# Turning blocks of an encoder's mixers by 32x32 squares through HBM in place of TensorE

## The chip, the core and the metric

The kernel runs on one core of a Trainium2 chip. The metric is the device time of one execution in microseconds (us); a comparison uses the median of several executions. The engines are TensorE (PE in the profile, its weight loads PEld), VectorE (DVE), ScalarE (ACT), GpSimd (POOL), and SyncE (SP), which here only issues transfers. Each engine works through its own queue in order; an instruction that waits holds up all that stands behind it on that engine.

## What is computed

A trunk of two layers over 256 tokens of width 2048, in float32. With `h = rms_norm(x)`, cut to what matters:

```python
# layer 0: retention (8 heads) and neighbourhood attention (8 heads), one input projection
rq, rk, rv, rg, nq, nk, nv = split(h @ w_in_ab, 7)
ret = rms_norm(retention(rq, rk, rv), ret_g) * silu(rg)
na = attention(rms_norm(nq, na_q_g), rms_norm(nk, na_k_g), nv, rpb)
x = x + concat(ret, na) @ w_out_ab
# layer 1: differential attention (8 heads, two softmax maps each)
q, k, v = split(h @ w_in_c, 3)
x = x + diff_attention(rms_norm(q, q_g), rms_norm(k, k_g), v) @ w_out_c
# both layers: 4-head cross-attention into 256 memory tokens, then a SwiGLU FFN of width 5632
k, v = split(rms_norm(mem) @ w_kv, 2);  q = rms_norm(x) @ w_q
x = x + attention(rms_norm(q, xq_g), rms_norm(k, xk_g), v) @ w_o
g, u = split(rms_norm(x) @ w_ffn_in, 2);  x = x + (silu(g) * u) @ w_ffn_out
```

## The kernel before

**Products.** Every large product is done by `gemm` (L297). A float32 operand is split into a high part that TensorE takes as it is (`hi`, `wh`) and a rest (`lo`, `wl`), and three matmuls make a product: `hi x wh`, `hi x wl`, `lo x wh` (L321 to L323). The stationary side is the activation with its features on the partitions, 16 k-tiles of 128 features by 256 tokens, as a `pair` of two tiles (L212). The moving side are the weights in blocks of 512 columns.

**The unit of work** is half a weight load: two k-tiles for two halves of the tokens, 12 matmuls of 512 columns. A block of 512 output columns takes 8 units when it contracts over 2048. `prepare` (L269) readies units ahead: SP loads a 1 MB block of weights into `raw` (three buffers, two units each), ScalarE casts it to `wh` (L292), VectorE subtracts to get `wl` (L293), three buffers of each. So a unit is cast when TensorE is done with the one three units earlier. All 864 units are in one list, so that weights of the next product are readied during the last units of the one before.

**The epilogues.** When a block's last unit is issued, `epi` takes its two accumulators (256 tokens on the partitions by 512 columns). For a query or a key with a norm, `normed_T` (L481): ScalarE squares (L470), VectorE sums by head (L471), POOL takes the power -1/2 (L334), VectorE scales to `z` (L475). For one without a norm, `plain_T` (L496): ScalarE copies with the token's scale (`evac`, L451). For a gate (L652, L653): silu and a product with the retention's output give `sg`. The accumulators have two buffers, so a block waits for the epilogue two blocks before.

**Turning.** What comes out has tokens on the partitions; scores and output projections need features there. TensorE turns a block of 512 features by `turn` (L340): four 128x128 transposes against an identity into one PSUM bank, twice for a block; after each, `gained_pair` (L442) on ScalarE (`hi`, times a gain) and VectorE (`lo`). `heads_T` (L459) does it for queries and keys, `gate_T` (L607) for the gates. A second way is `regroup` (L377), used before the change for the residual stream (`feed`, L409) and for the FFN's activations (`act_T`, L830): VectorE transposes 32x32 squares within the partitions (L389, two instructions), SP stores the 512 KB to a buffer `zd` in HBM (L391), POOL loads it back in four pieces that put the squares in their places (L394), and ScalarE and VectorE split it into `hi` and `lo`.

**The order by hand.** Everything beside the units is a generator in `Side` (L33). After each unit `pump` runs one step (in two of the products, two) of the first task in the list that is due; a step's `yield n` sets it due n units later. At most `CAP` tasks are begun and unfinished at a time. `drain` runs tasks until the given ones are done, where a product needs their output. In `regroup` the loads come `LAND` = 2 units after the squares, and the splitting `MOVE` = 5 units after them. A key's or query's turn comes 4 units after its epilogue, a plain one's 3, a gate's 2. Heads (`attend` L548, `ret_head` L581, `diff_head` L662) start when the queries and the keys of their group are both turned.

**Order of blocks.** Neighbourhood groups (query, key, value blocks, twice), retention groups (twice), two gate blocks; in layer 1 four groups of query, key and value. The first two blocks of a mixer are woven into each other, so that they end two units apart; from the third on a block follows the other. In the cross-attention the memory's keys come first, then the queries, then the values.

**Buffers.** Large pairs live in two places, A and B, that change roles: `hT` in one and the mixer's output `oT` in the other. `qT` and `kT` are turned queries and keys, `m8` a shared place for the bias, the retention's output and the cross-attention's output.

Of the kernel before, what the change touches and what calls it, by code (L numbers as in the profile page):

```python
# [16 lines left out]
P = 128  # L17
# [8 lines left out]
NEG = -1e30  # L26
LAND, MOVE = 2, 5
FFN_GROUPS = ((0, 4), (4, 8), (8, 11))
# [4 lines left out]
class Side:  # L33

    CAP = 5

# [43 lines left out]
def trunk_kernel(  # L82
# [214 lines left out]
    def gemm(kts, src, epi, gate=None, steps=1, wide=False):  # L297
        hi, lo = src
        w2, rows, cols, order = plan[at["phase"]]
# [3 lines left out]
        for b, u in order:  # L303
# [13 lines left out]
            for t in range(2):  # L317
                ts = slice(t * P, (t + 1) * P)
                for j in range(2):
                    kt = kts[u // 2] + 2 * (u % 2) + j  # L320
                    nc.tensor.matmul(acc[t], lhsT=hi[:, kt, ts], rhs=wh[:, j], start=first and j == 0, stop=False)  # L321
                    nc.tensor.matmul(acc[t], lhsT=hi[:, kt, ts], rhs=wl[:, j], start=False, stop=False)  # L322
                    nc.tensor.matmul(acc[t], lhsT=lo[:, kt, ts], rhs=wh[:, j], start=False, stop=last and j == 1)  # L323
            if last:
# [23 lines left out]
    def gained(dst, kt, src, g):  # L348
        hi, lo = dst[0][:, kt], dst[1][:, kt]
# [26 lines left out]

    def regroup(srcs, room=""):  # L377


        if room == "m8":  # L380
            both = m8.tile([P, 2, 4 * T], F32, tag="m8", name="zz")
            zt, zT = both[:, 0], both[:, 1]
        elif room:
            zt, zT = (qk.tile([P, 4 * T], F32, tag=room + x, name="zz") for x in "hl")
        else:
            zt, zT = (vp.tile([P, 4 * T], F32, tag="v" + x, name="zz") for x in "hl")
        zt = zt.rearrange("p (j k t b) -> p j k t b", j=4, k=4, t=2)
        for t in range(2):
            nc.vector.transpose(zt[:, :, :, t], srcs[t].rearrange("p (k j a) -> p j k a", j=4, a=32))  # L389
        zd = dram.tile([4, 32, 4, T], F32, name="zd")  # L390
        nc.sync.dma_start(zd.rearrange("i a j n -> (i a) (j n)"), zt.rearrange("p j k t b -> p (j k t b)"))  # L391
# [17 lines left out]
    def feed(dst, b, srcs, gi, layer, ssr, room):  # L409
# [5 lines left out]
        for k in range(4):  # L415
            g = gain(gi, layer, 4 * b + k)
            hi, lo = (x[:, 4 * b + k].rearrange("p (t i b) -> p t i b", t=2, i=4) for x in dst)
# [6 lines left out]
    def feed_x(dst, b, gi, layer, ssr, room=""):  # L424

        return [side.add(feed(dst, b, x_block(b), gi, layer, ssr, room))] * 2
# [31 lines left out]

    def heads_T(zs, dst, g):  # L459
        for u in range(2):  # L460
# [19 lines left out]

    def normed_T(acc, rstd, gc, name, wait=4):  # L481
        r1, r2 = rstd
# [10 lines left out]
        d = turned(name)  # L493
        return d, side.add(heads_T(zs, d, head_gain(gc)), wait)

    def plain_T(acc, rstd, name, mul):  # L496
        zs = evac(acc, rstd)
        d = turned(name)
        return d, side.add(heads_T(zs, d, mul), 3)

# [47 lines left out]
    def attend(g, h, dst, kt, bias=None):  # L548
# [15 lines left out]
        for s in range(2):  # L564
            product(po, part(v, s, slice(h * HD, (h + 1) * HD)), part(pT, s), s == 0, s == 1)
        split(dst[0][:, kt], dst[1][:, kt], po)

# [38 lines left out]

    def gate_T(zs, oT, kt, g):  # L607
        for u in range(2):
            pt = turn(zs, u)
            gained_pair(part(oT, slice(kt + 2 * u, kt + 2 * u + 2)), pt, g)  # L610
            yield 0

    def retention_na(j, hT, rstd, oT, gate):
        groups = [{"n": 0} for gi in range(4)]
        groups[0]["tb"] = side.add(na_bias(j, 0, groups[0], hT[0][:, 4, 0:16].bitcast(F32)), 6)
        tails = []

        def epi(b, acc):
            if b < 12:
                gi, part = b // 3, b % 3  # L620
                g = groups[gi]
                if gi < 2:
                    if part == 0:
                        g["q"], g["tq"] = normed_T(acc, rstd, c_naq + j, "qT")
                    elif part == 1:
                        g["k"], g["tk"] = normed_T(acc, rstd, c_nak + j, "kT")
                        side.drain([g["tb"], small[0]])
                        heads = [side.add(attend(g, h, oT, 8 + gi * 4 + h, bias=g["bias"]), cond=prepared(g))
                                 for h in range(4)]
# [15 lines left out]
            else:  # L645
# [4 lines left out]
                for t in range(2):  # L650
# [108 lines left out]
    for layer in range(2):  # L759
# [36 lines left out]
        ssr = new_ss("ssx")  # L796
        tasks = [t for b in range(4) for t in feed_x(hT, b, 1, layer, ssr, ("", "", "qT", "m8")[b])]
# [14 lines left out]
        xo = m8.tile([P, 2, 4, T], F32R, tag="m8", name="xo")  # L812
        xo = (xo[:, 0], xo[:, 1])
        heads = [side.add(attend(g, h, xo, h), cond=prepared(g)) for h in range(4)]
# [5 lines left out]
        def epi_xo(b, acc):  # L820
# [3 lines left out]
            else:  # L824
                tasks.extend(feed_x(hT, b, 3, layer, ssr, ("", "", "qT", "kT")[b]))

# [3 lines left out]
        def act_T(aT, zs, kt):  # L830
            zT = yield from regroup(zs)
            for t in range(2):
                split(*(x[:, kt:kt + 4, t * P:(t + 1) * P].rearrange("p k (i b) -> p k i b", i=4) for x in aT),
                      zT[:, :, :, t].rearrange("p i k b -> p k i b"))

# [75 lines left out]
```

## Time and profile before

| | |
|---|---|
| median of 3 runs | 2475.36 us (2473.93 to 2477.48) |
| the profiled execution | 2475.84 us |
| its span, first to last instruction | 2474.1 us |
| TensorE, share of the span busy | 99% |
| VectorE, ScalarE, POOL | 60%, 48%, 6% |
| transfers, mean share of 16 DMA engines busy | 4 to 8 tenths in the slices of the page |
| moved | 511.82 MB, 207 GB/s |

How to read its rows: "L345 PE MATMUL pt<-ident,z" is line, engine, operation, tile written and tiles read. Behind a group stand its count, its busy time in us, the mean in ns of one instruction, and the idle time of the engine just before, with what ended it. A row of the timeline begins with its start and its length in us (two merged instructions, x2, have one length for both). A row of waits is: engine and line, what it waited for, then us in all, times, the longest. Matmuls overlap in the pipeline, so their lengths are longer than the steps between their starts. The lines that matter most here are L345 (turns), L389 to L394 (squares) and L292/L293 (weights).

### The profile page before, as it was taken

The numbers are of one execution on the slowest core, as the hardware profiler recorded it, in microseconds if no ns is written. First come the engines' busy times: TensorE is split into PE (matmuls) and PEld (weight loads), VectorE is DVE, ScalarE is ACT, GpSimd is POOL, SyncE is SP. The second block draws the span as 40 slices with busy tenths as digits, with TensorE's granted clock in tenths as the row PEclk, the third lists the DMA queues.
The fourth block names the chain that finished last, engine by engine and source line by source line (L and its number), as shares of the span: only waits on it lengthen the run. The fifth ranks groups of instructions, "written<-read, shape, count | busy, mean of one in ns | idle before, by whom it ended". The sixth has DMA issues, their size and how long they took to land.

```text
span 2474.1 us, 28641 instructions
## 1 busy us (share of the span) xinstructions
PE 2456.3 (99%) x11184; PEld 2037.1 (82%) x11184; DVE 1475.7 (60%) x1833; ACT 1187.0 (48%) x1538; POOL 138.2 (6%) x215
## 2 busy tenths in 40 slices
PE   8999999999999999999999999999999999999999
PEld 6888888888888888888888888888888888888887
DVE  6775565675655555555567766767655545555554
ACT  6554464564443444444455555655544444443443
POOL 1000001010000000000010000010100000000000
PEclk9999999999999999999999999999999999999999
DMA  8555567656765666566674555675766656665665
GB/s 288 177 169 179 175 226 245 214 192 213 233 216 200 205 212 225 194 198 226 225 241 164 170 170 168 212 249 171 237 222 210 215 188 214 228 206 200 207 217 175
DMA packets 250184, 511.82 MB, mean 207 GB/s; under 512 B 11328, under 2 KB 11968, under 8 KB 250048
## 3 DMA queue, kind: packets, MB, share of 16 engines
q1 hardware_dynamic: 239568, 484.47, 58.5%
q0 software_dynamic: 8320, 23.08, 4.1%
q10 hardware_dynamic: 2160, 2.44, 0.3%
q8 instruction: 87, 1.43, 0.2%
q14 instruction: 49, 0.40, 0.0%
HBM read 486.88 MB, written 23.07 MB: 206 GB/s over the span
## 4 chain that ended last, share of the span: by engine, by line
PE 92%; DMA 3%; DVE 3%; ACT 1%; POOL 1%; issue 0%; ACTq 0%; SPq 0%; POOLq 0%; DVEq 0%
PE acc L322 30%; PE acc L321 30%; PE acc L323 30%; DMA zz<-zd 2%; DVE wl L293 1%; DMA zd<-zz 1%; PE pt L345 1%; ACT wh L292 0%; PE pt L545 0%; PE pa_s L437 0%; PE pa_s L436 0%; DVE x_sb L741 0%; PE pa_s L435 0%; POOL zz L394 0%; PE pa_r L595 0%
## 5 line engine op out<-in xcount | busy, mean ns | idle before, releaser
L293 DVE TENSOR_TENSOR wl<-raw,wh 128x1024 fp32r<-128x1024 f32 (+1 forms) x865 | 1053.7, 1221 | 870.8 <-ACT wh L292 870.4
L292 ACT CAST wh<-raw 128x1024 fp32r<-128x1024 f32 (+1 forms) x865 | 909.1, 1051 | 1158.2 <-PE acc L323 1132.8
L322 PE MATMUL acc<-wl,hTfh 128*128 128x512 f32 x1408 | 547.9, 389 | 0.6 <-DVE wl L293 0.6
L323 PE MATMUL acc<-wh,hTfl 128*128 128x512 f32 x1408 | 547.7, 389 | 0.0
L321 PE MATMUL acc<-wh,hTfh 128*128 128x512 f32 x1408 | 547.7, 389 | 0.0
L321 PE MATMUL acc<-wh,hTh 128*128 128x512 f32 x832 | 332.0, 399 | 9.8 <-ACT wh L292 8.3
L322 PE MATMUL acc<-wl,hTh 128*128 128x512 f32 x832 | 325.7, 391 | 0.9 <-DVE wl L293 0.9
L323 PE MATMUL acc<-wh,hTl 128*128 128x512 f32 x832 | 325.8, 392 | 0.0
L322 PEld LDWEIGHTS acc<-wl,hTfh 128*128 128x128 f32 x1408 | 264.3, 188 | 56.2 <-DVE wl L293 1.4
L323 PEld LDWEIGHTS acc<-wh,hTfl 128*128 128x128 f32 x1408 | 264.3, 188 | 54.9
L321 PEld LDWEIGHTS acc<-wh,hTfh 128*128 128x128 f32 x1408 | 264.3, 188 | 54.9
L322 PE MATMUL acc<-wl,aTh 128*128 128x512 f32 x704 | 274.0, 389 | 0.2 <-DVE wl L293 0.2
L323 PE MATMUL acc<-wh,aTl 128*128 128x512 f32 x704 | 273.9, 389 | 0.0
L321 PE MATMUL acc<-wh,aTh 128*128 128x512 f32 x704 | 273.9, 389 | 0.0
L321 PEld LDWEIGHTS acc<-wh,hTh 128*128 128x128 f32 x832 | 157.2, 189 | 40.0 <-ACT wh L292 8.3
L323 PEld LDWEIGHTS acc<-wh,hTl 128*128 128x128 f32 x832 | 156.7, 188 | 34.0
L322 PEld LDWEIGHTS acc<-wl,hTh 128*128 128x128 f32 x832 | 157.2, 189 | 31.2 <-DVE wl L293 1.8
L394 POOL DMA_DIRECT2D zz<-zd x160 | 87.3, 552 | 1589.9 <-DMA zd<-zz 1410.9
L322 PEld LDWEIGHTS acc<-wl,aTh 128*128 128x128 f32 x704 | 132.1, 188 | 28.2 <-DVE wl L293 0.8
L321 PEld LDWEIGHTS acc<-wh,aTh 128*128 128x128 f32 x704 | 132.1, 188 | 27.5
L323 PEld LDWEIGHTS acc<-wh,aTl 128*128 128x128 f32 x704 | 132.1, 188 | 27.3
L321 PE MATMUL acc<-wh,oTh 128*128 128x512 f32 x256 | 100.2, 392 | 0.0
(189 smaller groups left out, 1940.3 us busy)
## 6 DMA issues: line engine op xcount, KB each, us to landing
raw<-in_w_ffn_in SPq DMA_DIRECT2D x176, 1024.0 KB, 5.1
raw<-in_w_ffn_out SPq DMA_DIRECT2D x88, 1024.0 KB, 5.1
raw<-in_w_in_ab SPq DMA_DIRECT2D x55, 1024.0 KB, 5.2
raw<-in_w_in_c SPq DMA_DIRECT2D x48, 1024.0 KB, 5.2
zd<-zz SPq DMA_DIRECT2D x40, 512.0 KB, 3.8
zz<-zd POOLq DMA_DIRECT2D x160, 128.0 KB, 5.4
raw<-in_w_out_ab SPq DMA_DIRECT2D x16, 1024.0 KB, 5.1
raw<-in_w_xkv SPq DMA_DIRECT2D x16, 1024.0 KB, 5.0
```

Source lines behind the costliest of these rows:

```text
L292: nc.scalar.copy(wh[:, js], raw[:, rs])
L293: nc.vector.tensor_sub(wl[:, js], raw[:, rs], wh[:, js])
L321: nc.tensor.matmul(acc[t], lhsT=hi[:, kt, ts], rhs=wh[:, j], start=first and j == 0, stop=False)
L322: nc.tensor.matmul(acc[t], lhsT=hi[:, kt, ts], rhs=wl[:, j], start=False, stop=False)
L323: nc.tensor.matmul(acc[t], lhsT=lo[:, kt, ts], rhs=wh[:, j], start=False, stop=last and j == 1)
L345: nc.tensor.transpose(pt[:, j, t * P:(t + 1) * P], srcs[t][:, c:c + P], ident)
L394: nc.gpsimd.dma_start(zT[32 * j:32 * j + 32].rearrange("a (i n) -> a i n", i=4), zd[:, :, j].rearrange("i a n -> a i n"))
```

## The change

Twelve blocks go from `turn` to `regroup`: the neighbourhood queries (2), the retention queries (2), the differential queries (4), the gates (2) and the memory's keys (one in each layer). The other keys, the cross-attention's queries, the probabilities and the heads' outputs are still turned by TensorE.

- The moved blocks begin in the step right after their epilogue (a wait of 0 in place of 4, 3 or 2 units), and their splitting comes `SLOW` = 8 units after the squares; where there is a gain, ScalarE multiplies the landed block by it in place first. The loads still come after 2 units.
- The squares lie in a free place: for the mixers' queries the block of the output pair that is written last or not yet (`oT`'s block 0 in layer 0, block 3 in layer 1), for the gates `qT` and `kT`, for the memory's keys `qT`.
- So that a quarter of a pair can be lent, a pair becomes four blocks of four k-tiles, each a tile of its own (`Pair`), and the kernel addresses k-tiles by `at`.
- `CAP` goes from 5 to 6 tasks.

```diff
-LAND, MOVE = 2, 5
+LAND, MOVE, SLOW = 2, 5, 8
...
-    CAP = 5
+    CAP = 6
...
-    def pair(which, name):
-        hi = big.tile([P, 16, T], F32R, tag=f"{which}h", name=f"{name}h")
-        lo = big.tile([P, 16, T], F32R, tag=f"{which}l", name=f"{name}l")
-        return hi, lo
+    class Pair:
...
+        def __init__(self, which, name):
+            self.which, self.name, self.blocks = which, name, {}
+
+        def blk(self, b):
+            if b not in self.blocks:
+                self.blocks[b] = tuple(big.tile([P, 4, T], F32R, tag=f"{self.which}{x}{b}", name=f"{self.name}{x}")
+                                       for x in "hl")
+            return self.blocks[b]
+
+        def at(self, kt, n=None):
+            k = kt % 4
+            return tuple(x[:, k if n is None else slice(k, k + n)] for x in self.blk(kt // 4))
...
+    def room_for(room):
...
+        if room in ("qT", "kT"):
+            return tuple(qk.tile([P, 4 * T], F32, tag=room + x, name="zz") for x in "hl")
+        return tuple(big.tile([P, 4 * T], F32, tag=room[0] + x + room[1], name="zz") for x in "hl")
+
+    def regroup(srcs, room="v", wait=MOVE):
...
         yield LAND
         for j in range(4):
             nc.gpsimd.dma_start(zT[32 * j:32 * j + 32].rearrange("a (i n) -> a i n", i=4),
                                 zd[:, :, j].rearrange("i a n -> a i n"))
-        yield MOVE - LAND
+        yield wait - LAND
         return zT.rearrange("p (i k t b) -> p i k t b", i=4, k=4, t=2)
+
+    def split_moved(dst, zT):
+
+        for t in range(2):
+            split(*(x[:, :, t * P:(t + 1) * P].rearrange("p k (i b) -> p k i b", i=4) for x in dst),
+                  zT[:, :, :, t].rearrange("p i k b -> p k i b"))
...
-    def heads_T(zs, dst, g):
+    def heads_T(zs, dst, g, room=None):
+        if room:
+            zT = yield from regroup(zs, room, wait=SLOW)
+            if g is not None:
+                flat = zT.rearrange("p i k t b -> p (i k t b)")
+                nc.scalar.activation(flat, flat, AF.Copy, scale=g)
+            split_moved(dst, zT)
+            return
         for u in range(2):
             pt = turn(zs, u)
             gained_pair(part(dst, slice(2 * u, 2 * u + 2)), pt, g)
...
-        return d, side.add(heads_T(zs, d, head_gain(gc)), wait)
+        return d, side.add(heads_T(zs, d, head_gain(gc), room), 0 if room else 4)
...
-        return d, side.add(heads_T(zs, d, mul), 3)
+        return d, side.add(heads_T(zs, d, mul, room), 0 if room else 3)
...
-    def gate_T(zs, oT, kt, g):
-        for u in range(2):
-            pt = turn(zs, u)
-            gained_pair(part(oT, slice(kt + 2 * u, kt + 2 * u + 2)), pt, g)
-            yield 0
+    def gate_T(zs, oT, kt, g, room):
+        yield from heads_T(zs, oT.at(kt, 4), g, room)
...
+        spare = oT.which + "0"
...
-                        g["q"], g["tq"] = normed_T(acc, rstd, c_naq + j, "qT")
+                        g["q"], g["tq"] = normed_T(acc, rstd, c_naq + j, "qT", spare)
...
-                    g["q"], g["tq"] = plain_T(acc, rstd, "qT", 1.0)
+                    g["q"], g["tq"] = plain_T(acc, rstd, "qT", None, spare)
...
-                tails.append(side.add(gate_T(zs, oT, gi * 4, head_gain(c_ret + j)), 2))
+                tails.append(side.add(gate_T(zs, oT, gi * 4, head_gain(c_ret + j), ("qT", "kT")[gi])))
...
+        spare = oT.which + "3"
...
-                g["q"], g["tq"] = normed_T(acc, rstd, c_dq + j, "qT")
+                g["q"], g["tq"] = normed_T(acc, rstd, c_dq + j, "qT", spare)
...
-            g["k"], g["tk"] = normed_T(acc, mssr[1:], c_xk + layer, "kT")
+            g["k"], g["tk"] = normed_T(acc, mssr[1:], c_xk + layer, "kT", "qT")
```

More of the change, by code (lines that the diff above doesn't have):

```diff
@@ L319, in gemm @@
                 for j in range(2):
[L320 to L323, printed above, removed]
+                    hi, lo = src.at(kts[u // 2] + 2 * (u % 2) + j)
+                    nc.tensor.matmul(acc[t], lhsT=hi[:, ts], rhs=wh[:, j], start=first and j == 0, stop=False)
+                    nc.tensor.matmul(acc[t], lhsT=hi[:, ts], rhs=wl[:, j], start=False, stop=False)
+                    nc.tensor.matmul(acc[t], lhsT=lo[:, ts], rhs=wh[:, j], start=False, stop=last and j == 1)
             if last:
@@ L479, in turned, with normed_T @@
         return tuple(qk.tile([P, 4, T], F32R, name=name + x) for x in "hl")
-    def normed_T(acc, rstd, gc, name, wait=4):
+    def normed_T(acc, rstd, gc, name, room=None):
         r1, r2 = rstd
@@ L627, in epi @@
                         side.drain([g["tb"], small[0]])
-                        heads = [side.add(attend(g, h, oT, 8 + gi * 4 + h, bias=g["bias"]), cond=prepared(g))
+                        heads = [side.add(attend(g, h, oT, 8 + gi * 4 + h, g["bias"]), cond=prepared(g))
                                  for h in range(4)]
@@ L796, in trunk_kernel @@
         ssr = new_ss("ssx")
-        tasks = [t for b in range(4) for t in feed_x(hT, b, 1, layer, ssr, ("", "", "qT", "m8")[b])]
+        tasks = [t for b in range(4) for t in feed_x(hT, b, 1, layer, ssr, ("v", "v", "qT", "m8")[b])]
         g = {"wait": 3}
         def epi_k(b, acc):
-            g["k"], g["tk"] = normed_T(acc, mssr[1:], c_xk + layer, "kT")
+            g["k"], g["tk"] = normed_T(acc, mssr[1:], c_xk + layer, "kT", "qT")
         def epi_q(b, acc):
@@ L812, in trunk_kernel @@
         xo = m8.tile([P, 2, 4, T], F32R, tag="m8", name="xo")
-        xo = (xo[:, 0], xo[:, 1])
+        heads_out = pair("", "xo")
+        heads_out.blocks[0] = (xo[:, 0], xo[:, 1])
+        xo = heads_out
         heads = [side.add(attend(g, h, xo, h), cond=prepared(g)) for h in range(4)]
@@ L824, in epi_xo @@
             else:
-                tasks.extend(feed_x(hT, b, 3, layer, ssr, ("", "", "qT", "kT")[b]))
+                tasks.extend(feed_x(hT, b, 3, layer, ssr, ("v", "v", "qT", "kT")[b]))
         gemm((0,), xo, epi_xo, gate={0: heads[:2], 1: heads[2:]}, steps=2)
@@ L831, in act_T @@
             zT = yield from regroup(zs)
-            for t in range(2):
-                split(*(x[:, kt:kt + 4, t * P:(t + 1) * P].rearrange("p k (i b) -> p k i b", i=4) for x in aT),
-                      zT[:, :, :, t].rearrange("p i k b -> p k i b"))
+            split_moved(aT.at(kt, 4), zT)
         for g0, g1 in FFN_GROUPS:
```

30 lines of the change are left out of this document (14 added, 16 removed).

## The prediction

> **What bounds the kernel now.** I read the page's busy times first, then the chain that ended last, then what TensorE waited for, and only then single places in the timeline. From the page, part 1 and part 4:
>
> ```profile
> PE 2456.3 (99%) x11184; PEld 2037.1 (82%) x11184; DVE 1475.7 (60%) x1833; ACT 1187.0 (48%) x1538; POOL 138.2 (6%) x215
> ...
> PE 92%; DMA 3%; DVE 3%; ACT 1%; POOL 1%; issue 0%; ACTq 0%; SPq 0%; POOLq 0%; DVEq 0%
> ```
>
> TensorE is busy 99% of the span and carries 92% of the chain. Of the waits of its weight loads, the largest that comes more than once:
>
> ```profile
> PEld acc L322 <- DVE wl L293: 5.0, 7, 0.9
> ```
>
> So its weight loads wait for VectorE's `wl`, the low halves of the weights, 5.0 us in 7 places, and no more. An instruction taken off TensorE shortens the run by what it holds TensorE, as long as `wl` does not get late in its place. That condition is what this prediction is about. How the weights pace ScalarE, by its timeline:
>
> ```profile
> 1364.41 1.05 ACT L292 CAST wh<-raw 128x1024 fp32r<-128x1024 f32 x1 [1.18 <-PE acc L323]
> 1367.13 1.05 ACT L292 CAST wh<-raw 128x1024 fp32r<-128x1024 f32 x1 [1.67 <-PE acc L323]
> ```
>
> A cast starts when TensorE frees a buffer, every 2.72 us: one unit of 12 matmuls, so 0.227 us a matmul. Beside its cast ScalarE has 1.67 us free in a unit.
>
> **What goes.** The turns by TensorE, by the view of line 345:
>
> ```profile
> L345 PE MATMUL pt<-ident,z x160: 270/272/273, 58.9 to 1706.1; 128*128 128x128 f32 x160
> L345 PEld LDWEIGHTS pt<-ident,sg x16: 138/140/142, 337.0 to 363.4; 128*128 128x128 f32 x16
> L345 PE MATMUL pt<-ident,sg x16: 270/272/273, 337.2 to 363.5; 128*128 128x128 f32 x16
> ```
>
> These durations overlap in the pipeline, so what a group of four costs is read from TensorE's timeline around one (a query of the differential layer):
>
> ```profile
> 1369.42 0.39 PE L323 MATMUL acc<-wh,hTl 128*128 128x512 f32 x1
> 1369.65 0.60 PE L345 MATMUL pt<-ident,z 128*128 128x128 f32 x4
> 1370.01 0.48 PE L321 MATMUL acc<-wh,hTh 128*128 128x512 f32 x1
> 1370.32 0.39 PE L322 MATMUL acc<-wl,hTh 128*128 128x512 f32 x1
> ```
>
> From L323 to the next unit's L322 pass 0.90 us; two undisturbed steps are 0.45 us; the group costs 0.45 us (0.447 before rounding). The change moves twelve blocks: neighbourhood queries 2, retention queries 2, differential queries 4, gates 2, memory keys 2. Each is two groups of four: 24 groups, 96 of these 176 transposes. **Saved on TensorE: 24 x 0.447 = 10.7 us.**
>
> **What comes.** The nearest rows are those of the activations, which take this very way already:
>
> ```profile
> L389 DVE STREAM_TRANSPOSE zz<-sg 128x512 f32<-128x512 f32 x44 | 28.5, 685 | 0.0
> L430 DVE TENSOR_TENSOR aTl<-zz,aTh 128x512 fp32r<-128x512 f32 x44 | 28.3, 685 | 0.0
> ...
> L447 DVE SCALAR_TENSOR_TENSOR kTl<-pt,gcol,kTh 128x512 fp32r<-128x512 f32 x16 | 11.9, 745 | 0.0
> ```
>
> A moved block gives VectorE two square transposes (685 ns) and two subtractions (685) for two fused ones (745): 2.74 for 1.49 us, 15 us more in the whole run. ScalarE gets two casts in place of two copies, and with a gain one pass over 128x1024 more, whose price I take from the cast of that size, 1.05 us (the rows at 1364.41). SP gets 12 stores, POOL 48 loads. In sum all of this fits: VectorE is 60% busy, ScalarE 48%. What matters is when it comes.
>
> Of the moved blocks, eight come out of a head norm (neighbourhood and differential queries, memory keys). There VectorE stands still for POOL's power, then scales `z`, then has weights to catch up on. VectorE at the place of the four rows above:
>
> ```profile
> 1366.95 1.29 DVE L475 TENSOR_TENSOR z<-acc,rr 128x512 f32<-128x512 f32 x2
> 1368.16 2.35 DVE L293 TENSOR_TENSOR wl<-raw,wh 128x1024 fp32r<-128x1024 f32 x2
> ```
>
> The first `wl` was ready from 1365.46 (its cast above) and went behind `z`, which comes earlier in the program. The new square transposes are issued in the step right after the epilogue, ahead of these weights in the program too. Do they also go ahead of them on VectorE? The feed-forward part shows the same meeting; ScalarE's cast, then VectorE:
>
> ```profile
> 631.41 1.06 ACT L292 CAST wh<-raw 128x1024 fp32r<-128x1024 f32 x1 [1.67 <-PE acc L323]
> ```
>
> ```profile
> 632.24 1.29 DVE L389 STREAM_TRANSPOSE zz<-sg 128x512 f32<-128x512 f32 x2
> 633.46 1.18 DVE L293 TENSOR_TENSOR wl<-raw,wh 128x1024 fp32r<-128x1024 f32 x1
> ```
>
> The weights were ready at 632.47, yet both transposes went first. I take that order, and 1.29 us for the pair.
>
> - *Differential queries, second to fourth block.* The first `wl` ends at 1368.16 + 1.22 = 1369.38 now and 1.29 later then, 1370.67. TensorE, without the turn, wants it at 1370.32 - 0.45 = 1369.87. It waits 0.80 us; three times: 2.4 us. In the run before it had 0.94 us to spare here. So a query saves 0.89 and gives 0.80 back.
> - *First query of each mixer.* Its block and the keys' block end two units apart, and the keys' `z` is pushed back as well. VectorE's weights behind the keys' `z`, and TensorE's use of them:
>
> ```profile
> 1316.30 2.35 DVE L293 TENSOR_TENSOR wl<-raw,wh 128x1024 fp32r<-128x1024 f32 x2
> ```
>
> ```profile
> 1318.00 0.39 PE L322 MATMUL acc<-wl,hTh 128*128 128x512 f32 x1
> ```
>
> The end, 1317.52, moves by +1.29 and by about -0.66 (a fused subtraction of the query that stood before it): 1318.15. TensorE would be two groups earlier, at 1317.11: 1.0 us. For the neighbourhood mixer's first query I take the same: 2.1 us together.
> - *Second neighbourhood query.* VectorE and TensorE:
>
> ```profile
> 117.50 2.35 DVE L293 TENSOR_TENSOR wl<-raw,wh 128x1024 fp32r<-128x1024 f32 x2
> ```
>
> ```profile
> 120.16 0.39 PE L322 MATMUL acc<-wl,hTh 128*128 128x512 f32 x1
> ```
>
> 118.72 + 1.29 = 120.01 against 119.71: 0.3 us.
> - *Memory keys.* In the first layer VectorE's `wl` behind the keys' `z`, then TensorE in both layers:
>
> ```profile
> 473.77 1.22 DVE L293 TENSOR_TENSOR wl<-raw,wh 128x1024 fp32r<-128x1024 f32 x1
> ```
>
> ```profile
> 475.37 0.39 PE L322 MATMUL acc<-wl,hTxh 128*128 128x512 f32 x1
> ...
> 1682.72 0.50 PE L322 MATMUL acc<-wl,hTxh 128*128 128x512 f32 x1 [0.49 <-DVE wl L293]
> ```
>
> 474.99 + 1.29 = 476.28 against 475.37: 0.9 us. In the second layer TensorE waits there already, so all of 1.29 is added. Together 2.2 us.
> - *Retention queries and gates.* No power, no catching up; VectorE idles ahead of its weights where the first retention query ends:
>
> ```profile
> 187.66 1.23 DVE L293 TENSOR_TENSOR wl<-raw,wh 128x1024 fp32r<-128x1024 f32 x1 [1.42 <-ACT wh L292]
> ```
>
> The pair fits into that; 0, and TensorE's 4 x 0.89 us stay saved.
>
> **Returned at the squares: 2.4 + 2.1 + 0.3 + 2.2 = 7.0 us.** Bounds: 0 (rival A), and 12 x 1.29 = 15.5 us if every pair delays TensorE in full, which would end at 2481.
>
> The landing half comes eight units later, 21.8 us, about where the keys' epilogue stands. ScalarE needs 1.05 + 1.05 us there, VectorE 1.37. The weights are cast up to three units ahead, so I take it as mostly hidden: 0 where no epilogue stands, 0.25 us at the four sequential queries that meet their keys' epilogue, 1.0 us in all. Bounds: 0, and 10 blocks with a gain x 1.05 = 10.5 us if the extra pass is hidden nowhere. Heads start when queries and keys are both there; keys still take their turn after 8 + 4 units, so heads move only in the first blocks, by two units, and TensorE fills that with weights: 0. The smaller buffers (four k-tiles each) let early blocks be overwritten sooner: 0, since TensorE's waits are so few that nothing is there to win. SP's weight loads stand behind a store that waits for VectorE; three weight buffers cover it: 0.
>
> **Sum:** 2475.84 (the profiled execution, 1.7 us beyond its span) - 10.7 + 7.0 + 1.0 = 2473.1. That execution was 0.48 us above the median 2475.36, so **2472.7**, 0.1% faster. A difference under 0.2% (5 us) is no change to this measurement. Own range of this case: 2469.5 to 2476.5.
>
> By the Trainium skill, page "VectorE: DVE Perf Modes", section "Rules for kernel authors", a 128x128 transpose belongs on TensorE when PSUM can take the result, and VectorE's is for 32x32 within a bank. Its table in "The three transpose paths" has 390 ns against 311 ns for a 128x128 bf16 tile; the rows above, 0.447 us for four on TensorE against 1.29 us for the pair on VectorE, lean further to that side, and by that rule nothing would be gained.
>
> **Rivals.**
>
> *A: everything saved stays saved.* Should the squares be put behind the waiting weights, or VectorE find the time, only the 1.0 us is paid: 2472.7 - 7.0 = 2465.7. For it: VectorE is idle 40% of the run. Against it: the order at 632.24, and `z` itself ahead of ready weights. Chance 0.30. The Trainium skill, page "Perfetto Trace Analysis", section "Identifying the Most-Contended Engine", says to optimise the engine with the highest occupancy first; read plainly, that is this rival. The 99% row agrees with the choice of engine.
>
> *B: slower, by landings that come late.* The first ScalarE instruction of a landing waits for POOL's four loads, with the weights' casts queued behind it, and for these TensorE. From the chain, a burst of transfers and a quieter one:
>
> ```profile
> 541.06 6.83 DMA zd<-zz
> ...
> 550.08 9.15 DMA zz<-zd
> ...
> 1661.81 3.31 DMA zd<-zz
> ...
> 1667.29 6.96 DMA zz<-zd
> ```
>
> Store to last landing: 18.2 and 12.4 us. The epilogue of the query above begins on ScalarE at
>
> ```profile
> 1360.38 0.60 ACT L470 ACTIVATE sq<-acc 128x512 f32<-128x512 f32 x1 [0.47 <-PE acc L323]
> ```
>
> and its squares would be done at 1369.5, 9.2 us later (9.3 with the store's issue). So it lands after 21.7 or 27.5 us, against 21.8. Quiet ones are just in time. A crowded one leaves ScalarE waiting 5.7 us, of which some 3.1 us are covered by weights ahead (two units, 5.44, less a cast of 1.05 and a `wl` of 1.22): 2.6 us lost. Three of the eight normed blocks late decide for slower; four give 2472.7 + 10.4 = 2483. Against it: weights load at an even pace inside a mixer. Chance 0.15.
>
> *C: it does not do what it says at the heads.* If queries arrive after their keys everywhere, heads crowd into the values' epilogue, VectorE's weights slip there, and the last 2.7 us are lost: 2475.4. Chance 0.09.
>
> **How the numbers follow.** Forecast 0.46, of which 0.05 reaches below 2470.4; A 0.30; B 0.15; C 0.09. Faster 0.35, same 0.50, slower 0.15. The range takes in A with an us below it and part of B: 2464.5 to 2481.
>
> **What would show it.** Right: 80 transposes of `z` and none of `sg` left on line 345; VectorE's order `z`, `zz`, `wl` at the normed blocks; 8 new TensorE waits for `wl` of 0.3 to 1.3 us; none at retention queries and gates. Wrong towards A: `wl` ahead of `zz`. Wrong towards B: ScalarE waiting for the load of `zz` ahead of a `qT` or `kT` instruction, by more than 3 us.

## The result, and the profile after

| | before | after |
|---|---|---|
| median | 2475.36 us | 2490.62 us (2489.09 to 2492.56, 5 runs) |
| ratio to before | | 1.0061, interval 1.0049 to 1.0072 |
| span of the profiled execution | 2474.1 us | 2488.2 us |

Slower by 0.61%, 15 us, where 2472.7 was forecast. Parts 1 and 4 of the page after:

```profile
PE 2455.2 (99%) x11088; PEld 2030.3 (82%) x11088; DVE 1489.0 (60%) x1857; ACT 1197.5 (48%) x1548; POOL 168.3 (7%) x263
...
PE 86%; DMA 5%; DVE 4%; issue 3%; POOL 2%; ACT 1%; ACTq 0%; POOLq 0%; DVEq 0%
```

The work went off TensorE as meant, 96 matmuls fewer. But its share of the chain fell from 92% to 86%; transfers, VectorE, POOL and issue (3%, time in which nothing that the profile shows was waited for) took the rest. The view of TensorE's turns (now line 358), then the waits of ScalarE, TensorE and its weight loads:

```profile
L358 PE MATMUL pt<-ident,z x80: 270/272/332, 66.1 to 1719.8; 128*128 128x128 f32 x80
```

```profile
ACT zz L488 <- DMA zz<-zd: 22.6, 7, 5.3
...
PE acc L335 <- DVE wl L307: 7.7, 13, 1.0
PE pt L358 <- DVE z L506: 5.6, 12, 1.3
...
PEld acc L335 <- DVE wl L307: 14.3, 17, 1.4
```

Three things to see. ScalarE stands still 22.6 us in seven places for the loads of moved blocks (line 488 is the gain in place). The arrival of a moved block, with its gain pass and its two casts on ScalarE, is called a landing from here on. The weight loads' waits for `wl` grew from 5.0 to 14.3 us. And there is one that the view of before did not list: the turn of a key that stays on TensorE waits for its `z`.

One such place in full, the fourth differential query and its keys. ScalarE:

```profile
1517.10 0.60 ACT L501 ACTIVATE sq<-acc 128x512 f32<-128x512 f32 x1 [0.46 <-PE acc L336]
...
1535.61 1.06 ACT L306 CAST wh<-raw 128x1024 fp32r<-128x1024 f32 x1 [1.66 <-PE acc L336]
1540.77 1.15 ACT L488 ACTIVATE zz<-zz,gcol 128x1024 f32<-128x1024 f32 x1 [4.10 <-DMA zz<-zd]
1541.95 0.62 ACT L453 CAST qTh<-zz 128x512 fp32r<-128x512 f32 x1
1542.48 1.05 ACT L306 CAST wh<-raw 128x1024 fp32r<-128x1024 f32 x1
1543.43 0.61 ACT L453 CAST qTh<-zz 128x512 fp32r<-128x512 f32 x1
1543.95 0.59 ACT L501 ACTIVATE sq<-acc 128x512 f32<-128x512 f32 x1
```

The first row is the query's epilogue, the last the keys'. Between them in the queue stand the wait of 4.10 us, the landing (1.15, 0.62, 0.61 us) and a late cast. TensorE behind it:

```profile
1543.58 0.49 PE L334 MATMUL acc<-wh,hTh 128*128 128x512 f32 x1
1544.84 0.50 PE L335 MATMUL acc<-wl,hTh 128*128 128x512 f32 x1 [0.76 <-DVE wl L307]
...
1550.94 0.30 PE L358 MATMUL pt<-ident,z 128*128 128x128 f32 x1 [0.60 <-DVE z L506]
1551.45 0.55 PE L358 MATMUL pt<-ident,z 128*128 128x128 f32 x3 [0.21 <-DVE z L506]
```

It pays twice: once for weights that were cast late, and 6 us on for the keys' `z`, whose chain (squares, sums, POOL's power, scaling) began late. By the starts of its units it lost 1.2 us in the first and 1.2 in the second, and 0.6 more behind it, where the next `wl` stood behind that late `z` on VectorE.

The table below shows where time went. It compares the traces by the start of the same unit's first matmul: kernel minus before, in us. Each column is one execution, and the profiled ones lie between 3.0 us above their kernel's median (pin_8) and 2.1 below it (eight), so single entries are not good to a microsecond or two. The kernels of the columns are described below.

| unit, start before | after | land_free | no_squares | slow_11 | pin_8 | pin_11 | sq_tied | best | eight |
|---|---|---|---|---|---|---|---|---|---|
| 432, 1240.5 | 3.3 | 1.6 | 4.0 | 0.2 | 5.1 | 0.2 | 1.2 | -1.9 | -5.1 |
| 448, 1285.4 | 3.5 | 0.7 | 3.3 | 0.4 | 4.5 | 0.1 | 0.8 | 0.8 | -5.2 |
| 552, 1608.4 | 9.5 | 1.4 | 1.8 | 5.8 | 10.3 | 0.6 | -2.1 | -2.1 | -8.1 |
| 608, 1773.5 | 13.1 | -0.9 | -0.6 | 10.8 | 8.8 | -0.1 | -2.4 | -3.5 | -9.6 |

Units 448 to 552 hold the differential mixer, 552 to 608 the second memory keys, what stands ahead of 432 the first layer. In the mixer four queries save 3.6 us (8 groups of 0.447). After lost 6.0 there instead, so 9.6 came back where the prediction had some 4.2 (3.4 at the squares, three times 0.25 at landings). At the second memory keys it lost another 3.6 where 0.9 should have been saved. ScalarE there, the first and the last row being the squares of the cross-attention's queries:

```profile
1703.80 0.60 ACT L501 ACTIVATE sq<-acc 128x512 f32<-128x512 f32 x1 [0.30 <-PE acc L336]
1709.58 1.15 ACT L488 ACTIVATE zz<-zz,gcol 128x1024 f32<-128x1024 f32 x1 [5.18 <-DMA zz<-zd]
1710.63 1.03 ACT L306 CAST wh<-raw 128x1024 fp32r<-128x1024 f32 x1
1711.57 0.59 ACT L501 ACTIVATE sq<-acc 128x512 f32<-128x512 f32 x1
```

A landing waited for in the middle of an epilogue: the two squares are 7.8 us apart, 2.3 in the kernel before.

The first layer gave back as much as the mixer. Seven of its blocks are moved, which should save 6.3 us; after stood 3.3 later, so 9.6 came back, where the prediction had 2.2 (squares) and next to nothing else. With the landings out of the products (land_free, below) 7.9 of it still came back.

### The profile page after: what moved, and what is told of

The parts are those of the page before. It is cut to its first block, busy times and chain, and to the rows that moved or that the text cites. A ratio compares the mean times of both kernels' runs of the same rounds, so it can differ in the third digit from the quotient of the medians.

```text
span 2488.2 us, 28609 instructions
## 1 busy us (share of the span) xinstructions
PE 2455.2 (99%) x11088; PEld 2030.3 (82%) x11088; DVE 1489.0 (60%) x1857; ACT 1197.5 (48%) x1548; POOL 168.3 (7%) x263
## 4 chain that ended last, share of the span: by engine, by line
PE 86%; DMA 5%; DVE 4%; issue 3%; POOL 2%; ACT 1%; ACTq 0%; POOLq 0%; DVEq 0%
PE acc L335 28%; PE acc L336 27%; PE acc L334 27%; DMA zz<-zd 3%; DVE wl L307 2%; POOL rr L347 1%; DMA zd<-zz 1%; DMA x_sb<-in_x 1%; POOL zz L412 1%; ACT wh L306 1%; DVE z L506 0%; DVE ss L502 0%; PE pt L358 0%; PE pa_s L461 0%; PE pa_s L460 0%
## 5 line engine op out<-in xcount | busy, mean ns | idle before, releaser
L412 POOL DMA_DIRECT2D zz<-zd x208 | 114.3, 556 | 1696.7 <-DMA zd<-zz 1324.7
```

## The experiments

All were timed beside the kernel before, whose median was 2475.05, 2475.34, 2475.92 and 2475.86 us in the four sets. The theories in the first set are L (landings come late: the prediction's rival B), S (squares cost more than thought), H (the first heads, which start when a group's queries and keys are both turned).

**land_free.** The split reads the squares' tile, not the loaded block; stores and loads still run. So the rearranging by HBM does not reach the products.

```diff
+        if wait == SLOW:
+            zT = zt
         return zT.rearrange("p (i k t b) -> p i k t b", i=4, k=4, t=2)
```

> Theory L (late landings: ScalarE's first instruction of a landing waits for POOL's loads, with the casts of the weights queued behind it). Theory S (squares: VectorE's two square transposes stand ahead of weights that TensorE wants). Theory H (heads: queries that are there later than their keys push the heads, and what hangs on them, into the next epilogue). In this kernel the twelve moved blocks still make their squares, store and load them, but are split from the squares before the round trip, so nothing computes with what the loads bring and nothing waits for them; its output is not the reference's. In the changed kernel's trace I count some 14 us of TensorE's losses at late landings, 6 at squares, 5.5 where the first neighbourhood heads meet the lambdas. L expects 2474 to 2479 us; S and H, where L is not the cause, 2487 to 2491.

Measured 2473.39 us, ratio 0.9993 (0.9984 to 1.0001). 17 us of the loss hang on the landings, with all the traffic still there; in the table it is 14.0 by unit 608, of it 5.3 in the mixer, 5.9 at the second memory keys, 1.7 in the first layer and 1.0 between units 432 and 448. It doesn't say by what means: here the split also stands much nearer to the squares in the queue (at the fourth query it begins 4.2 us behind them, in after 15.9).

**no_squares.** The twelve blocks are stored as they are, in two stores, with the squares on VectorE left out.

```diff
-        for t in range(2):
-            nc.vector.transpose(zv[:, :, :, t], ...)
...
+        if wait == SLOW:
+            for t in range(2):
+                nc.sync.dma_start(flat[:, t * NB:(t + 1) * NB], srcs[t])
```

> The twelve moved blocks are stored as they are, without VectorE's square transposes (24 instructions less), by two stores of 256 KB in place of one of 512 KB; what is loaded back is not in the right places, so its output is not the reference's. S expects the 6 us at the squares back and a little at the landings, which begin 1.3 us earlier: 2482 to 2486 us. L expects only the latter, 2486 to 2490. H: no change.

Measured 2476.27, ratio 1.0003 (0.9994 to 1.0012): better than either theory had it. Its ScalarE still waits for landings, as long as after's:

```profile
ACT zz L493 <- DMA zz<-zd: 24.2, 9, 4.4
```

At the fourth query:

```profile
1531.90 1.15 ACT L493 ACTIVATE zz<-zz,gcol 128x1024 f32<-128x1024 f32 x1 [3.92 <-DMA zz<-zd]
...
1536.03 0.59 ACT L506 ACTIVATE sq<-acc 128x512 f32<-128x512 f32 x1
```

A wait of 3.92 us, as in after, and TensorE lost 1.2 us against 3.0 (the step of the table's quantity from unit 528 to 536). What differs is where the keys' epilogue stands behind it: 4.1 us behind the gain pass, with two casts between, in after 3.2 us, with one. The wait as such isn't the loss; this run told the theories apart that are set up below (Q and E).

**slow_11.** Three units more of slack; the first gate is finished in the next product, not by a drain.

```diff
-LAND, MOVE, SLOW = 2, 5, 8
+LAND, MOVE, SLOW = 2, 5, 11
...
-        side.drain(tails[:1])
-        return {6: tails}
+        return {4: tails[:1], 6: tails}
```

> Eleven units in place of eight between the squares and the splitting, and the first gate is waited for at the fifth unit row of the output projection in place of at the end of the input projection. L expects the waits of ScalarE for loads to go and 8 to 14 us with them: 2477 to 2483 us. S expects no change. H expects the first heads of a mixer three units later still and 0 to 4 us on top of what the others give.

Measured 2486.99, ratio 1.0046 (1.0034 to 1.0059). L's number missed, and ScalarE still waits 21.4 us in eight places for landings. ScalarE at the fourth query shows why:

```profile
1514.96 0.59 ACT L501 ACTIVATE sq<-acc 128x512 f32<-128x512 f32 x1
...
1536.99 1.15 ACT L488 ACTIVATE zz<-zz,gcol 128x1024 f32<-128x1024 f32 x1 [4.09 <-DMA zz<-zd]
```

Between these rows stand six casts; in after, between 1517.10 and 1540.77, seven. The step in the program came three units later and the instruction did not: the order in the queue is not that of the program's steps. A `yield` is not a place in a queue, and the experiment did not test what it was meant to.

**plain_only.** Only the retention queries and the gates are moved (no `room` for the normed blocks).

> Only the retention queries and the gates take the way through HBM; neighbourhood and differential queries and the memory's keys go back to TensorE. The mixture of tiles and the six tasks stay. It saves 8 groups of four transposes, 3.6 us. S and H expect nothing against it: 2471 to 2473 us. L expects the loss of about 4 us at the first gate to stay: 2475 to 2477.

Measured 2475.46, ratio 0.9996 (0.9988 to 1.0005), in L's range. The saving of 3.6 us isn't seen. Both gates' landings are waited for, the first 5.9 us, and one retention query's 2.4:

```profile
ACT zz L488 <- DMA zz<-zd: 7.3, 2, 5.9
```

The second set ties a landing to its step by data: the gain pass takes its factor from a 128x1 copy that reads a late `wh`.

```diff
+        at["wh"] = wh
...
+                late = sm.tile([P, 1], F32, name="late")
+                nc.scalar.activation(late, at["wh"][:, 0, 0:1].bitcast(F32), AF.Identity, bias=g, scale=0.0)
-                nc.scalar.activation(flat, flat, AF.Copy, scale=g)
+                nc.scalar.activation(flat, flat, AF.Copy, scale=late)
```

**pin_8.** The tie alone, at eight units.

> The gain pass of a landing reads its factor from a 128x1 copy that ScalarE makes after the cast of the weights last prepared at that step, so the landing can't stand further ahead in ScalarE's queue than the step says; the landing itself, the squares and the eight units are those of the changed kernel. In the changed kernel the landing stands behind 7 casts counted from the query's squares of its sums, here behind 8: about one unit (2.7 us) later. Theory Q (place in ScalarE's queue: in the changed kernel ScalarE stood up to 5.3 us for a landing, 22.6 us in 7 places, with casts and the keys' squares behind it): the wait shrinks from about 4 to about 1.4 us each, half of the loss goes: 2477 to 2485. Rival W (the landing's own work and traffic cost the time, wherever it stands): no change, 2487 to 2492.

Measured 2482.29, ratio 1.003 (1.0018 to 1.0041). The number fits Q, the trace does not. The waits for landings are down to 3.6 us in two places; yet from unit 448 to 552 TensorE lost 5.7 us, as in after (6.0). ScalarE and TensorE at the fourth query:

```profile
1542.86 1.15 ACT L491 ACTIVATE zz<-zz,late 128x1024 f32<-128x1024 f32 x1 [2.18 <-DMA zz<-zd]
1543.91 0.58 ACT L504 ACTIVATE sq<-acc 128x512 f32<-128x512 f32 x1
1544.39 1.13 ACT L454 CAST qTh<-zz 128x512 fp32r<-128x512 f32 x2
1545.42 0.60 ACT L504 ACTIVATE sq<-acc 128x512 f32<-128x512 f32 x1
```

```profile
1552.32 0.30 PE L359 MATMUL pt<-ident,z 128*128 128x128 f32 x1 [1.27 <-DVE z L509]
```

One cast later in the queue, the landing now stands right in the keys' epilogue. With half the wait it costs TensorE the same, by the keys' turn. (What this trace gained over after is at the second memory keys: from unit 552 to 608 it stands 1.5 us better, after 3.6 worse. It is pin_8's slowest execution, 2485.25 us; what the median gained beyond it is not in the trace.)

**pin_11.** The tie at eleven units, with slow_11's gate.

> The same tie, with 11 units (and the first gate finished during the next product, as in slow_11). Against slow_11 it changes only the tie: there the landing still stood behind the same 6 to 7 casts, whatever the step said; here it stands behind 10 to 12, after the keys' squares. Theory Q: no landing is waited for, TensorE's loss at the landings goes: 2471 to 2477, ScalarE's waits for the load of zz under 6 us in all (22.6 in the changed kernel). Rival W: as slow_11, 2485 to 2489.

Measured 2475.38, ratio 1.0001 (0.9992 to 1.001). The tie is the only difference from slow_11, and 11.6 us are gone. ScalarE's keys' epilogue and the landing:

```profile
1533.62 0.60 ACT L504 ACTIVATE sq<-acc 128x512 f32<-128x512 f32 x1 [0.30 <-PE acc L337]
...
1535.93 0.59 ACT L504 ACTIVATE sq<-acc 128x512 f32<-128x512 f32 x1
...
1544.09 0.68 ACT L470 ACTIVATE kTh<-pt,gcol 128x512 fp32r<-128x512 f32 x1
1544.67 0.28 ACT L490 ACTIVATE late<-wh,gcol 128x1 f32<-128x1 f32 x1
1544.99 1.16 ACT L491 ACTIVATE zz<-zz,late 128x1024 f32<-128x1024 f32 x1
```

Same work, same transfers, behind the epilogue: rival W falls. So theory E, formed from these runs and so not foretold by any of them: a landing costs when it stands close ahead of, or in, the next block's epilogue on ScalarE, by its wait and its own 2.4 us together. Its four corners, by what came back in the differential mixer: after (wait and collision) 9.6 us, pin_8 (collision, less wait) 9.3, pin_11 (neither) 4.1, no_squares (wait, little collision) 2.0. In all but the last the squares have a share, 3.4 us by the run of sq_tied below; without it the four are 6.2, 5.9, 0.7 and 2.0. At the fourth query the delay of the keys' epilogue can be read directly, as the time from the query's first squares of sums to the keys', and set beside the step of the table's quantity from unit 528 to 536:

| | before | land_free | pin_11 | no_squares | slow_11 | pin_8 | after |
|---|---|---|---|---|---|---|---|
| ScalarE waited for the landing, us | | | 0 | 3.9 | 4.1 | 2.2 | 4.1 |
| query's squares to keys' squares, us | 22.7 | 22.6 | 23.2 | 24.0 | 24.5 | 25.9 | 26.9 |
| lost by TensorE, us | | 0.0 | -0.7 | 1.2 | 2.2 | 2.8 | 3.0 |

The loss goes with the second row, not with the first. The second memory keys are a second place, and it agrees: from unit 584 to 592 after lost 5.9 us and slow_11 6.7, where the landing stands between the queries' two squares; no_squares, whose landing is waited for 1.1 us but stands 4.7 us ahead of them, and land_free lost 0.0, pin_8 0.6 and pin_11 1.1.

**lam_split and pin_11_lam.** After and pin_11, with the row of lambdas used six units after its load.

```diff
             nc.scalar.dma_start(lrow[:, i, :], l.broadcast_to([P, HD]))
+        yield 6
...
-        return
-        yield
```

> The changed kernel with the lambdas used 6 units after the load, nothing else. Theory H: 2 to 4 us under the changed kernel, 2486.5 to 2488.5, and TensorE's stall before the first heads' products (4.4 us in the group at 107 us) back to 1 to 2 us. Theory Q has nothing to say on it: the landings of the differential queries and of the second memory's keys keep their waits of 3 to 5 us.

> pin_11, and in the first layer the row of lambdas is used 6 units after its load was issued, not in the same step. Theory H (VectorE waited 3.6 us for that load at 107 us, and TensorE's first heads behind it): 2 to 3 us under pin_11, and VectorE's wait for the row gone. If that place is covered by what is lost later anyway: within 1 us of pin_11.

Measured 2490.99 (1.0063, 1.005 to 1.0075) and 2475.94 (1.0004, 0.9995 to 1.0012): no change. But VectorE's wait in lam_split is there still, 3.3 us for 3.6 in after:

```profile
DVE lprod L203 <- DMA lrow<-in_lambda_k: 3.3, 1, 3.3
```

Again a `yield` did not do away with the wait (pin_11 has 1.5 us, pin_11_lam 1.2). So H is not refuted; it wasn't tried. Against it stands that the kernel before waits 2.9 us for the same row.

The third set splits up what pin_11 still gives back.

**sq_tied.** Squares of the normed blocks four units later, all squares tied behind a `wl`; landings eight units behind the squares; the tie of the landings and slow_11's gate as in pin_11.

```diff
+        at["wh"], at["wl"] = wh, wl
...
+        if wait == SLOW:
+            nc.vector.tensor_copy(zt[:, 0:33:32], at["wl"][:, 0, 0:2].bitcast(F32))
...
-        return d, side.add(heads_T(zs, d, head_gain(gc), room), 0 if room else 4)
+        return d, side.add(heads_T(zs, d, head_gain(gc), room), 4 if room else 4)
```

> pin_11 (2475.38), with the squares begun four units after the epilogue and tied behind the low half of the weights last prepared there: VectorE first writes two columns of the squares' tile from that low half. So on VectorE the squares stand behind two or three of the weights that wait for it, in place of ahead of them; the landing stands 8 units behind the squares, 12 behind the epilogue. Theory S (the prediction's term: the squares give back 7.0 us on TensorE at the eight normed blocks, since the weights are caught up behind them): 2468 to 2471. Theory S2 (in pin_11's trace only 4.0 us of TensorE's loss stand at the squares in the differential mixer, 1.3 to 2 of them at the keys' turn of the first group): 2471 to 2474. Rival M (what pin_11 returns lies elsewhere, in the heads of the cross-attention behind the late memory keys): within 1 us of pin_11.

Measured 2473.68, ratio 0.9992 (0.9983 to 1.0001), in S2's range; its interval and pin_11's overlap. VectorE in pin_11, then in sq_tied, at the fourth query:

```profile
1517.20 1.29 DVE L509 TENSOR_TENSOR z<-acc,rr 128x512 f32<-128x512 f32 x2
...
1518.80 1.29 DVE L408 STREAM_TRANSPOSE zz<-z 128x512 f32<-128x512 f32 x2
1520.02 3.45 DVE L307 TENSOR_TENSOR wl<-raw,wh 128x1024 fp32r<-128x1024 f32 x3
```

```profile
1515.51 1.29 DVE L511 TENSOR_TENSOR z<-acc,rr 128x512 f32<-128x512 f32 x2
...
1517.10 2.35 DVE L307 TENSOR_TENSOR wl<-raw,wh 128x1024 fp32r<-128x1024 f32 x2
...
1519.69 1.30 DVE L410 STREAM_TRANSPOSE zz<-z 128x512 f32<-128x512 f32 x2
```

Over the mixer the table's quantity moves by -2.9 in place of +0.5: squares ahead of the weights cost 3.4 us there. That step comes again: keys_turned and pin_11_lam, with pin_11's squares, move by +0.5, best and eight, with sq_tied's, by -2.9. The total gains less than that, since outside the mixer sq_tied loses 1.1 us more than pin_11 by unit 608.

**keys_turned.** pin_11 with the memory's keys on TensorE.

```diff
-            g["k"], g["tk"] = normed_T(acc, mssr[1:], c_xk + layer, "kT", "qT")
+            g["k"], g["tk"] = normed_T(acc, mssr[1:], c_xk + layer, "kT")
```

> pin_11 with the memory's keys turned by TensorE again, as before the change: ten blocks moved in place of twelve. TensorE pays 1.8 us more for the turns. Theory M (in pin_11 the keys of the memory land 4 to 5 us after the heads could start, and TensorE's heads of the first layer's cross-attention take 10.5 us over their matmuls in the group at 512 us, 5.4 in the changed kernel): 2472 to 2474, the group at 512 us back to 5.4 us. Without M: 2476.5 to 2478.

Measured 2475.10, ratio 0.9997 (0.9988 to 1.0006). In the first layer's cross-attention (units 160 to 184) the profiled pin_11 lost 3.4 us against before and keys_turned gained 0.5: late keys hold the heads. But the time lies between the two forecasts, level with pin_11's, so what the profile shows in that place isn't shown to be a gain.

**best.** sq_tied with the memory's keys on TensorE.

> sq_tied with the memory's keys turned by TensorE again. If S2 and M both hold: 2469 to 2472, faster than the kernel before by 0.1 to 0.25%. If neither: 2475 to 2478.

Measured 2472.97, ratio 0.9992 (0.9984 to 1.0001), between the two forecasts.

**eight.** best with the neighbourhood queries on TensorE too: retention queries, gates and differential queries remain moved.

> best with the neighbourhood queries, too, turned by TensorE as before the change: eight blocks moved (retention queries, gates, differential queries), landings and squares tied. In best, TensorE stands 2 us behind the kernel before until the retention's queries, with nothing left there of the 1.8 us that the two neighbourhood queries save: the first heads are shuffled by them. If these heads are what the neighbourhood queries cost: level with the kernel before until 200 us, then 3.6 us saved at retention queries and gates and 3 in the differential mixer: 2468.5 to 2472 and a ratio whose interval lies below 1. If the first heads are late for another reason (the block buffers, a sixth begun task): the same 2 us are lost, 2471 to 2475.

Measured 2468.80, ratio 0.9974 (0.9965 to 0.9983): faster than both kernels, by 7.06 us against before. Its chain, and its weight loads' wait for `wl`:

```profile
PE 97%; DMA 1%; DVE 1%; ACT 0%; POOL 0%; issue 0%; ACTq 0%; DVEq 0%; POOLq 0%
```

```profile
PEld acc L336 <- DVE wl L307: 2.9, 5, 0.8
```

Its 16 groups are worth 16 x 0.447 = 7.15 us on TensorE, so the sum agrees. By place it does so with some luck: the differential mixer gave 2.9 of its 3.6 us, the retention queries and gates 3.9 of 3.6, and the rest of the run 2.8 in this trace, with no block moved there; it is eight's fastest execution. Best stands 3.2 us behind eight at unit 432 and 6.1 at unit 448, far more than two queries' turns. Some 4 of it came between units 433 and 435 of best, behind a landing of the residual stream that the kernel before has too: ScalarE waited 5.5 us for it, and the granted clock was 0.52 from 1247 to 1250.4 us. The rest was not followed.

## Why the prediction was wrong, step by step

- **Saved, 10.7 us: right.** 80 turns of `z` are left and none of `sg`; eight's sum is in keeping with the price of a group.
- **The squares, 7.0 us: right where it was measured.** The order `z`, `zz`, `wl` came as read. In the differential mixer the prediction had 2.4 + 1.0 = 3.4 us; pin_11 against sq_tied gives 3.4. That the two agree to the tenth is luck: the prediction has 1.0 us at the first query and 0.8 at each of the others, the traces give 1.6, -0.3, 1.2 and 1.0 (split at units 472, 496 and 520). At the fourth query TensorE waited, in pin_11,

```profile
1521.25 0.50 PE L336 MATMUL acc<-wl,hTh 128*128 128x512 f32 x1 [0.74 <-DVE wl L307]
```

  where 0.80 was said. The neighbourhood's and the memory keys' shares weren't measured apart.
- **The landing half: the step that failed.** The prediction put it "mostly hidden: 0 where no epilogue stands, 0.25 us at the four sequential queries that meet their keys' epilogue, 1.0 us in all". Land_free puts it at 17 us in the whole run, 16 more than forecast, and the whole miss is 18 (2490.62 against 2472.7); in the mixer, after against pin_11, it is 5.5. Even the upper bound of 10.5 was too low, because it counted the gain pass alone. Three things were missing. First, the slack: "eight units later, 21.8 us" is a distance in the program. On ScalarE the landing was reached 19.6 us after the query's first squares (1517.10 to 1536.67), and three units more in the program did not move it in the queue. Second, the load: the last piece of the fourth query came 4.0 us after that, so 23.6 us behind the first squares, where a quiet case had been given as 21.7 and just in time. Of the 4 us 2.2 are the queue's (19.6 for 21.8), 1.9 the load's. Third, and most: what was queued behind the waiting instruction. The cover by weights held about as reckoned: the next cast came 4.2 us late (4.10 + 1.15 + 0.62 less the usual 1.67), 3.1 had been put down as covered, and TensorE stood 1.0 us (1543.58 to 1544.84, less a step of 0.227). The keys' squares were behind it too, their `z` came late, and TensorE's queue holds that turn at a fixed place. That second bill was in no term.
- **Retention queries and gates, nothing returned: wrong in the changed kernel, right in eight.** From unit 56 to unit 120 eight gained 3.9 us, against 3.6 saved; after lost 2.0, so 5.6 came back. The first gate's landing, waited for 5.3 us, is a part of it (unit 112 to 120: after lost 1.8 us, land_free and pin_8 gained 1.0). Land_free gained only 0.5 over the whole stretch, so landings are not all of it.
- **Heads, 0.** Not settled, and the open end of this account. In the first layer the 7.9 us that came back without landings are 5.7 more than the squares' 2.2, and no run isolates them. Traces point to the neighbourhood's first heads: between units 28 and 34 after lost 6.5 us and land_free 8.2, after both had been 3 ahead at unit 28; eight, with those queries on TensorE, lost 0.0. Late memory keys hold the heads in pin_11's profile; the medians don't show it. The wait for the lambdas' row at 107 us was not done away with by either attempt.
- **Rival B had the direction** and its sign in the trace (ScalarE waiting more than 3 us ahead of a `qT` or `kT` instruction), with a chance of 0.15 and a price of 2483. Against it stood that weights load at an even pace inside a mixer. The window from 1529 to 1541 us, ahead of the fourth query's landing (engines' busy times, granted clock, busy share of the 16 DMA engines, GB/s), then its transfers' issues with KB and median us to landing:

```profile
1529.00:1541.00 12.00, 12.00 (x55) 9.94 (x54) 4.24 (x4) 3.40 (x4) 2.23 (x4) 1.00 0.98 294
```

```profile
raw<-in_w_in_c SPq DMA_DIRECT2D x2, 1024.0 KB, 9.3
zz<-zd POOLq DMA_DIRECT2D x4, 128.0 KB, 8.5
```

  The DMA engines are busy 0.98 of these 12 us: two weight loads take 9.3 us and the four pieces 8.5 in the median, 5.2 each in the median of the whole run. This was a burst, in the middle of a mixer. The range stopped at 2481, under the rival's own price.
- **A comparison that was off.** Beside the Trainium skill's table the prediction set 0.447 us, one group of four and so half a block, against 1.29 us, the squares of a whole one; a block is 0.89 us on TensorE. And the lower of the table's two figures, 311 ns, is VectorE's, so the rows do not lean further to the table's side. No term of the sum used it.

## What to carry to other kernels

When work is moved from the bounding engine to a way with a wait in it, look for what stands behind that wait in its queue: here the next block's epilogue and, behind VectorE and POOL, the bounding engine's own queue. A delay written into the program isn't a place in the queue: read the place from the trace, and where it matters tie it by data (a 128x1 copy of 0.28 us was enough). Fewer moved blocks can save more: with the same ties, eight moved blocks gained 7 us where twelve gained some 2, with an interval that reaches no change; twelve without ties lost 15.

## What was not expected of the hardware

A stall of TensorE can cost more than its length. After's windows of the trace (busy times of PE, PEld, DVE, ACT and POOL; then the granted clock):

```profile
358.00:361.30 3.30, 1.80 (x7) 0.96 (x6) 2.44 (x4) 3.30 (x6) 0.00 (x0) 1.00 0.28 103
361.40:364.60 3.20, 3.20 (x9) 2.43 (x9) 3.20 (x6) 3.20 (x7) 0.00 (x0) 0.50 0.06 15
1706.00:1713.00 7.00, 5.08 (x23) 3.65 (x21) 1.31 (x2) 3.42 (x5) 0.00 (x0) 1.00 0.62 190
1713.40:1716.10 2.70, 2.70 (x7) 2.05 (x7) 2.60 (x6) 1.67 (x2) 1.14 (x1) 0.50 0.00 0
```

Behind a stretch with gaps the granted clock is 0.50 for about 3 us, and matmuls start every 0.43 us, not 0.227:

```profile
1713.99 0.63 PE L334 MATMUL acc<-wh,mTh 128*128 128x512 f32 x1
1714.42 0.63 PE L335 MATMUL acc<-wl,mTh 128*128 128x512 f32 x1
```

Seven to nine matmuls at 0.2 us more each are 1.4 to 1.8 us on top of the stall. After has three such stretches inside its span, the third from 112 to 115 us (granted clock 0.52), the kernel before none: by an estimate from these rows 4 to 5 us of the 15. The Trainium skill, page "TensorE: Matmul & The Clock Gate", Part 1, has the half clock follow an idle window of about 3.4 us and end after one of sustained work. The length of the slow stretch agrees. The condition is looser here: TensorE was busy 1.80 of 3.30 us ahead of the slow stretch at 361.4.
